# A streaming encoder trunk: product 7's bank read at once, the first loads in order of need, and two multiplications of the last unit on GpSimd

## The chip, the core and the metric

The kernel runs on one core of a Trainium2 chip. The metric is the device time of one launch in microseconds (us). The core's engines are TensorE (PE; PEld is its weight load), VectorE (DVE), ScalarE (ACT), GpSimd (POOL) and SyncE (SP), which issues most DMAs. They have their own instruction queues and wait for each other by semaphores. Products are summed in PSUM, in banks of 128x512 f32.

## The reference, cut to what matters

One layer of a trunk over 2048 prompt tokens and 32 sample tokens, width 1024, all in f32:

```
h  = rmsnorm(x, g_pre_mix);  z = h @ w_in             # u | q | f | i | g, 512 columns each
y  = concat(pool_mix(u), hgrn(q, f, i) * silu(g)) @ w_out
x1 = x + rmsnorm(y, g_post_mix)
h2 = rmsnorm(x1, g_pre_ffn)
f  = (silu(h2 @ w_gate) * (h2 @ w_up)) @ w_down        # 2816 hidden columns
x2 = x1 + rmsnorm(f, g_post_ffn)
rmsnorm(x, g) = x * rsqrt(mean(x*x) + 1e-6) * g
```

`pool_mix` is a trailing mean with a small product per group, `hgrn` a gated recurrence evaluated in chunks. Outputs are x2 of both groups and the last pool rows and states.

## The kernel before, in words

The prompt is worked in two halves of 1024 tokens, the samples with the second. Each f32 product is made of three matmuls of f32r operands: every operand is split in a part `hi` (a ScalarE cast) and a rest `lo` (a VectorE subtraction), and hi·hi, hi·lo and lo·hi are summed in one bank.

**The start.** `first_values` (L566) makes the i columns of z for the first half. Everything in it, on all engines, stands in program order (`tc.manual_schedule`, L1732); in the rest of the kernel only TensorE's order is written out, and a planner orders the other engines by its own costs. The function issues its loads on SP: channel block 0 of x (`xT`, in two halves), weight rows 0 and 1 (`wrow`), channel block 1, then for `kp` 1 to 3 two channel blocks (512 KB, `channel_load`, L445) and two blocks of weight rows (512 KB, `raw_rows2`, L257), then constants (L592) and token tiles (`xt`, L451). Each channel block is scaled and split (`unscaled`, L595 to 601), each weight block split, and TensorE makes four tiles of 12 matmuls in all per channel block. Between blocks 5 and 6 stand the `rb` products (L504): they spread the roots of the tokens' mean squares, which come from the token tiles by ScalarE (`sumsq`, L319), GpSimd (L325, L326) and VectorE (`dg`, L461).

**Gate and up.** `gate_up` (L1246) makes gate and up columns by seven products per matrix m, in the manner of Strassen-Winograd, with 22 matrices in each half, gate and up in turn. Products 1, 6, 5 and 3 sum on in one bank `M.x` (`gx`); product 7 opens the bank `M.y` (`gy`) and product 4 sums on in it. So the value that product 7 alone leaves in `M.y` has to be read before product 4, and what product 5 leaves in `M.x` before product 3. A matrix is `held` when `M.x` starts with product 1 (m under 4 or from 6 on); in the others the copy `p1` is added by hand. The order is written out in `order_of` (L1179): 7, 5, product 1 of the next matrix, 4, 3, 6, 2 in the common run, and at the end of the stage, for the last matrices a and b, products 6, 2, 7, 5, 4, 3 of a and b in turn. `later` (L1255) holds steps that are emitted at the beginning of the next product's step.

**Down.** `down` (L1544) takes the hidden columns through seven products again, adding to `acc` in SBUF. In the last group each finished half row of a token tile goes to `half_done` (L1583): sum of squares on ScalarE, and in the very last unit (`direct`) at once the multiplication by the norm weight, `fg`. When both halves are there, GpSimd makes the root (`rstd_of`, L323, L326) and `done` (L1605) scales, adds the residual and stores. The last unit's order is 6, 7, 5, 4, 2, 3: its second tile t + 4 is finished by products 5 and 4, its first tile t by 2 and 3.

Of the kernel before, what the change touches and what calls it, by code (L numbers as in the profile page):

```python
# [13 lines left out]
ALU = mybir.AluOpType  # L14
PSUM = bass.MemoryType.PSUM

P = 128
# [61 lines left out]
def body(tc, ins, outs, cst):  # L79
    nc = tc.nc  # L80
    ctx = ExitStack()
    with ctx:
# [9 lines left out]
        def ztile(name, shape=None, dt=F32):  # L92
            return UP.tile(shape or [P, SLOT], dt, tag="u", name=name)
# [13 lines left out]
        def t2(name, shape=None, dt=F32):  # L107
            return TP.tile(shape or [P, 512], dt, tag="t", name=name)
# [7 lines left out]
        x_t = ins["x_channels"].rearrange("(k p) t -> p k t", p=P)  # L116
        w_in = ins["w_in"][0]
# [72 lines left out]
        class Pace:  # L190
            t = 0.0
# [80 lines left out]
        def raws(n):  # L272
            its = Stream.items
            while Stream.nraw < min(n, len(its)):
                its[Stream.nraw] = its[Stream.nraw]()
                Stream.nraw += 1
# [146 lines left out]
        COL_Q, COL_F, COL_I, COL_G = 512, 1024, 1536, 2048  # L423
# [19 lines left out]
        def channel_load(S, tg, k, n):  # L443
            t0 = S.tok0 + tg * 512
            nc.sync.dma_start(out=S.xT[tg][k // 2][:, k % 2:k % 2 + n], in_=x_t[:, k:k + n, t0:t0 + 512])  # L445
# [120 lines left out]
        def first_values(S):  # L566
# [7 lines left out]
            front_loads(S)  # L574
            S.xT[0] = [ztile("xT", [P, 2, 512]) for _ in range(4)]
            for kp in range(4):
                if kp:
                    channel_load(S, 0, 2 * kp, 2)
                    raws(kp + 1)
                    continue  # L580
                x0 = x_t[:, 0, S.tok0:S.tok0 + 512]
                nc.sync.dma_start(out=S.xT[0][0][:, 0, 0:256], in_=x0[:, 0:256])
                raw = ztile("wrow", [P, 2 * 512])
                Stream.items[0] = lambda: raw
                for i in range(2):
                    nc.sync.dma_start(out=raw[:, i * 512:(i + 1) * 512], in_=w_in[i * P:(i + 1) * P, COL_I:COL_I + 512])
                    if i == 0:
                        nc.sync.dma_start(out=S.xT[0][0][:, 0, 256:512], in_=x0[:, 256:512])
                    else:
                        channel_load(S, 0, 1, 1)  # L590
                raws(1)
# [18 lines left out]
            raw = Stream.items[0]  # L610
# [12 lines left out]
            for k in range(0, KD, 2):  # L623
# [9 lines left out]
                for kk in range(2):  # L633
# [9 lines left out]
                    if k + kk == KD - 3:  # L643
                        later = scaled_channels(S, 1)
# [601 lines left out]
        def gate_up(S, on_last):  # L1246
# [8 lines left out]
            jobs, later, gs = [], [], {}  # L1255
# [55 lines left out]
            def product(M, p, ps, start):  # L1311
                while p not in S.F:
                    S.post[1].step()
                wf, F = M.f.pop(p), S.F[p]
                for k in (0, 2):
                    trios = [(*(wf[:, i, kk * P:(kk + 1) * P] for i in range(2)),
                              *(x[:, (kk % 2) * 512:(kk % 2) * 512 + 512] for x in F[kk // 2])) for kk in (k, k + 1)]
                    for n, (a, b) in enumerate(in_turn(trios)):
                        mm(ps, a, b, start and k == 0 and n == 0, k == 2 and n == 5, rcost(512), not start)
                        if n % 3 == 2:  # L1320
                            poll()

            def close(M, name):
                c = getattr(M, name)
                if M.gate is None:
                    later.append(lambda: nc.scalar.activation(c, c, AF.Silu))
                else:
                    nc.vector.tensor_tensor(c, c, getattr(M.gate, name), ALU.mult)
# [24 lines left out]
            def step(m, p):  # L1353
                M = mats[m]
                if p == 1:
                    M.gate = mats[m - 1] if m % 2 else None
                    M.x = mmbank("gx") if M.held else axbank("gw")
                    product(M, 1, M.x, True)
                    M.c11 = t2("c11")
                    nc.scalar.copy(M.c11, M.x)  # L1360
                    if not M.held:
                        M.p1, M.c11 = M.c11, t2("c11")
                elif p == 2:
                    if M.held:
                        z = axbank("gz")
                        product(M, 2, z, True)
                        nc.vector.tensor_tensor(M.c11, z, M.c11, ALU.add)
                        close(M, "c11")
                    else:
                        product(M, 2, M.x, False)  # L1370
                        if M.gate is None:
                            nc.scalar.activation(M.c11, M.x, AF.Silu)
                        else:
                            nc.vector.tensor_tensor(M.c11, M.x, M.gate.c11, ALU.mult)
                elif p == 6:
                    if not M.held:
                        M.x = mmbank("gx")
                    product(M, 6, M.x, not M.held)
                    M.c21 = t2("c21")
                    if M.held:  # L1380
                        nc.scalar.copy(M.c21, M.x)
                    else:
                        nc.vector.tensor_tensor(M.c21, M.x, M.p1, ALU.add)
                    if m == len(mats) - 1:
                        sampled([m - 1, m])
                elif p == 7:
                    M.y = axbank("gy")
                    product(M, 7, M.y, True)
                elif p == 5:
                    product(M, 5, M.x, False)  # L1390
                    M.c22 = t2("c22")
                    if M.held:
                        nc.scalar.copy(M.c22, M.x)
                    else:
                        nc.vector.tensor_tensor(M.c22, M.x, M.p1, ALU.add)
                    if m < LEAD:
                        if m % 2:
                            sampled([m - 1, m])
                    elif m < len(mats) - 2 and m % 2 == 0:
                        sampled([m, m + 1])  # L1400

                    def rest():
                        nc.vector.tensor_tensor(M.c22, M.y, M.c22, ALU.add)  # L1403
                        close(M, "c22")
                    later.append(rest)
                elif p == 4:
                    product(M, 4, M.y, False)
                    nc.vector.tensor_tensor(M.c21, M.y, M.c21, ALU.add)
                    close(M, "c21")
                else:  # L1410
                    product(M, 3, M.x, False)
                    M.c12 = t2("c12")
                    src = M.x
                    if not M.held:
                        src = M.c12
                        nc.vector.tensor_tensor(M.c12, M.x, M.p1, ALU.add)
                        M.p1 = None
                    if M.gate is None:
                        nc.scalar.activation(M.c12, src, AF.Silu)
                    else:  # L1420
                        nc.vector.tensor_tensor(M.c12, src, M.gate.c12, ALU.mult)
                        jobs.append(hidden(S, m // 2, [M.c11, M.c12, M.c21, M.c22]))
                        mats[m - 1] = mats[m] = None
# [62 lines left out]
        class Down:  # L1486
            w = [None] * len(GROUPS)
# [56 lines left out]
        def down(halves):  # L1544
# [6 lines left out]
            gpf = []  # L1551
# [31 lines left out]
            def half_done(t, dh, direct):  # L1583
                cs = slice(dh * 512, dh * 512 + 512)
                f = acc[t][:, cs]
                if t not in stats:
                    xh = None
                    if direct:
                        xh = ztile("x1r", [P, D])
                        nc.sync.dma_start(out=xh, in_=x1_rows(t * P, P))  # L1590
                    stats[t] = [new_stat(), [], xh, [t2("fg") for _ in range(2)] if direct else None]
                st, seen, xh, fg = stats[t]
                sumsq(f, P, st[:, dh:dh + 1])
                seen.append(dh)
                if direct:
                    nc.vector.tensor_tensor(fg[dh], f, gpf[0][:, cs], ALU.mult)
                if len(seen) == 1:
                    first_half(st, P, dh)
                else:
                    rstd_of(st, P, True, nc.gpsimd, dh)  # L1600
                    for i in range(2):
                        wait = 1 if direct else i + (3 if t % 8 > 3 else 4)
                        pending.append((slot[0] + wait, lambda i=i: done(t, direct, i)))
# [192 lines left out]
```

## Time and profile before

| what | value |
|---|---|
| timed runs | median 2088.18 us (2087.85 to 2088.67, 3 runs) |
| profiled execution, own time | 2086.21 us |
| its span, first to last instruction | 2084.4 us |
| mean granted TensorE clock | 0.998 |
| PE / DVE / ACT / POOL busy | 99% / 68% / 40% / 14% |
| DMA | 321.06 MB, mean 154 GB/s |

The span is cut by stage: the first values until about 53 us, heads, pools and projection of the first half until 377, its gate and up until 800, the second half's mixers until 1187, its gate and up until 1640, down until 2075, and the tail. In the rows, a line reads start, duration, engine, line, operation, `out<-in`, shapes; what stands in brackets is the idle time before it and what ended it. TensorE's matmuls all carry line L199, that of a helper, so they are told apart by tile: `vps` first values, `rb` roots, `gx`, `gy`, `gz` gate and up, `dx`, `dy`, `dz` down.

### The profile page before, as it was taken

Reading aid. Unit: us, or ns where it says so; the run is one execution under the profiler, and the core shown is the slowest. Engines: PE = TensorE matmul, PEld = TensorE weight load, DVE = VectorE, ACT = ScalarE, POOL = GpSimd, SP = SyncE. Lnnn points to the kernel's source line nnn. Section 1 sums busy time; section 2 is a strip of 40 time slices with the busy share of each in tenths; the row PEclk is TensorE's granted clock in tenths of the full one; section 3 lists DMA queues with packets and bytes.
Section 4 is the critical chain, followed back from the end, with each engine's and each line's share of the span. In section 5 each row is a group of like instructions: output and inputs, shape, how many; then the busy total and the mean of one; then the engine's idle time right before and its main releaser. Section 6 shows DMA issues by size and latency. Waiting matters only on the chain.

```text
span 2084.4 us, 34134 instructions
## 1 busy us (share of the span) xinstructions
PE 2071.4 (99%) x13112; PEld 1689.0 (81%) x13112; DVE 1423.6 (68%) x2303; ACT 830.7 (40%) x1661; POOL 281.9 (14%) x387
## 2 busy tenths in 40 slices
PE   9999999999999999999999999999999999999998
PEld 8788888888888888788888788888888778888876
DVE  6566765787776778365575697776666766566587
ACT  6444445654444445233334563444444521011032
POOL 1133302100000000122231200000000210110133
PEclk9999999999999999999999999999999999999999
DMA  9321144435555558211014614554445796776778
GB/s 326 112 72 52 45 142 144 150 115 174 157 162 147 158 171 262 72 46 36 25 54 174 202 50 138 163 149 144 142 138 171 237 326 208 216 225 207 213 225 213
DMA packets 393361, 321.06 MB, mean 154 GB/s; under 512 B 18128, under 2 KB 320720, under 8 KB 393200
## 3 DMA queue, kind: packets, MB, share of 16 engines
q1 hardware_dynamic: 390752, 310.98, 48.1%
q0 software_dynamic: 2016, 7.34, 1.9%
q8 instruction: 103, 1.69, 0.3%
q10 hardware_dynamic: 432, 0.57, 0.1%
q14 instruction: 58, 0.48, 0.1%
HBM read 218.36 MB, written 100.47 MB: 153 GB/s over the span
## 4 chain that ended last, share of the span: by engine, by line
PE 94%; DVE 3%; issue 1%; ACT 1%; DMA 0%; POOL 0%; SPq 0%; DVEq 0%; POOLq 0%; ACTq 0%
PE gx L199 22%; PE mmb L199 16%; PE gy L199 11%; PE dx L199 10%; PE ops L199 10%; PE gz L199 5%; PE dy L199 5%; PE vps L199 4%; PE dz L199 3%; PE gb L199 1%; PE gw L199 1%; PE gsps L199 1%; DVE acc L1581 1%; PE ups L199 1%; PE tps L342 1%
## 5 line engine op out<-in xcount | busy, mean ns | idle before, releaser
L199 PE MATMUL gx<-fhi,wf 128*128 128x512 f32 x1376 | 387.0, 391 | 0.0
L199 PEld LDWEIGHTS gx<-fhi,wf 128*128 128x128 f32 x1376 | 256.7, 188 | 55.0 <-issue 2.2
L199 PE MATMUL gx<-flo,wf 128*128 128x512 f32 x688 | 213.1, 390 | 0.0
L199 PE MATMUL gy<-fhi,wf 128*128 128x512 f32 x704 | 201.6, 390 | 1.0 <-DVE c L1403 1.0
L199 PE MATMUL dx<-dhi,hst 128*128 128x512 f32 x640 | 185.3, 391 | 1.0 <-DVE acc L1581 0.9
L199 PE MATMUL mmb<-hTlo,whi 128*128 128x512 f32 x512 | 176.3, 405 | 0.0
L199 PE MATMUL mmb<-hThi,whi 128*128 128x512 f32 x512 | 165.8, 405 | 0.0
L1581 DVE TENSOR_TENSOR acc<-dx,acc 128x512 f32<-128x512 f32 x168 | 115.0, 689 | 71.3 <-PE dx L199 70.3
L199 PE MATMUL mmb<-hThi,wlo 128*128 128x512 f32 x512 | 159.0, 392 | 0.0
L1301 DVE TENSOR_TENSOR wf<-s,wf 128x512 fp32r<-128x512 f32 x176 | 119.7, 687 | 56.1 <-ACT wf L1296 54.2
L199 PEld LDWEIGHTS gy<-fhi,wf 128*128 128x128 f32 x704 | 131.8, 188 | 29.1 <-DVE c L1403 1.4
L199 PEld LDWEIGHTS gx<-flo,wf 128*128 128x128 f32 x688 | 129.1, 188 | 27.0
L1296 ACT CAST wf<-s 128x512 fp32r<-128x512 f32 x176 | 107.9, 621 | 102.3 <-DVE s L1277 31.5
L199 PEld LDWEIGHTS dx<-dhi,hst 128*128 128x128 f32 x640 | 119.6, 188 | 30.2 <-issue 3.4
L1520 ACT CAST dhi<-t 128x1024 fp32r<-128x1024 f32 x20 | 20.7, 1053 | 250.7 <-DVE dlo L1521 182.4
L1301 DVE TENSOR_TENSOR wf<-wraw,wf 128x512 fp32r<-128x512 f32 x132 | 89.6, 686 | 34.4 <-ACT wf L1296 34.4
L199 PEld LDWEIGHTS mmb<-hTlo,whi 128*128 128x128 f32 x512 | 96.2, 188 | 20.8 <-issue 1.3
L199 PEld LDWEIGHTS mmb<-hThi,wlo 128*128 128x128 f32 x512 | 96.3, 188 | 19.3 <-issue 0.7
L1296 ACT CAST wf<-wraw 128x512 fp32r<-128x512 f32 x132 | 80.7, 621 | 76.0 <-PE gx L199 36.3
L199 PEld LDWEIGHTS mmb<-hThi,whi 128*128 128x128 f32 x512 | 91.8, 188 | 21.1 <-issue 3.8
L199 PE MATMUL gy<-flo,wf 128*128 128x512 f32 x352 | 108.7, 389 | 0.0
L199 PE MATMUL dx<-dlo,hst 128*128 128x512 f32 x320 | 98.7, 389 | 0.0
(333 smaller groups left out, 3995.0 us busy)
## 6 DMA issues: line engine op xcount, KB each, us to landing
hst<-hdFalse SPq DMA_DIRECT2D x140, 256.0 KB, 2.9
hst<-hdTrue SPq DMA_DIRECT2D x140, 256.0 KB, 2.9
wraw<-in_w_gate_dram SPq DMA_DIRECT2D x50, 512.0 KB, 4.0
wraw<-in_w_up_dram SPq DMA_DIRECT2D x50, 512.0 KB, 4.0
hdFalse<-hhi SPq DMA_DIRECT2D x77, 256.0 KB, 2.3
hdFalse<-hlo SPq DMA_DIRECT2D x77, 256.0 KB, 2.3
hdTrue<-hhi SPq DMA_DIRECT2D x77, 256.0 KB, 2.6
hdTrue<-hlo SPq DMA_DIRECT2D x77, 256.0 KB, 2.6
```

The lines of the kernel that those rows point to most:

```text
L199: nc.tensor.matmul(out, l, r, start=start, stop=stop, skip_group_check=more)
L342: nc.tensor.transpose(ps[:, c:c + P], xn[:, (2 * kp + kk) * P:(2 * kp + kk + 1) * P], ident)
L1296: nc.scalar.copy(wf[:, 0], getattr(M, src) if isinstance(src, str) else src)
L1301: nc.vector.tensor_tensor(wf[:, 1], getattr(M, src) if isinstance(src, str) else src, wf[:, 0].bitcast(F32), ALU.subtract)
L1520: nc.scalar.copy(hi, src)
L1581: nc.vector.tensor_tensor(dst, ps, dst, ALU.add)
```

## The change

Three edits. In `first_values` the loads of `kp` 1 are issued as four DMAs of 256 KB in the order channel block 2, weight block 2, channel block 3, weight block 3, and GpSimd copies one column into the destination of three DMAs first, from a block that has to have landed: weight block 0 before channel block 2, weight block 1 before channel block 3, channel block 1 before channel blocks 4 and 5. As the DMA writes over that column, it is held until the copy is done. In `gate_up` `c22` is begun after product 7 from `M.y`, and `M.x` is added to it after product 5; the deferred `rest` is gone. In `half_done` the `fg` of tiles with t % 8 > 3 (in the last unit the second tile) goes from VectorE to GpSimd.

```diff
--- before.py
+++ after.py
@@ -574,7 +574,21 @@
             front_loads(S)
             S.xT[0] = [ztile("xT", [P, 2, 512]) for _ in range(4)]
             for kp in range(4):
+                if kp == 1:
+
+                    raw = ztile("wrow", [P, 2 * 512])
+                    Stream.items[1] = lambda: raw
+                    seen = Stream.items[0][:, 0:1], Stream.items[0][:, 512:513]
+                    for i in range(2):
+                        x, w = S.xT[0][1][:, i], raw[:, i * 512:(i + 1) * 512]
+                        nc.gpsimd.tensor_copy(x[:, 0:1], seen[i])
+                        nc.sync.dma_start(out=x, in_=x_t[:, 2 + i, S.tok0:S.tok0 + 512])
+                        nc.sync.dma_start(out=w, in_=w_in[(2 + i) * P:(3 + i) * P, COL_I:COL_I + 512])
+                    raws(2)
+                    continue
                 if kp:
+                    if kp == 2:
+                        nc.gpsimd.tensor_copy(S.xT[0][2][:, 0, 0:1], S.xT[0][0][:, 1, 0:1])
                     channel_load(S, 0, 2 * kp, 2)
                     raws(kp + 1)
                     continue
@@ -1386,23 +1400,20 @@
                 elif p == 7:
                     M.y = axbank("gy")
                     product(M, 7, M.y, True)
+                    M.c22 = t2("c22")
+                    if M.held:
+                        nc.scalar.copy(M.c22, M.y)
+                    else:
+                        nc.vector.tensor_tensor(M.c22, M.y, M.p1, ALU.add)
                 elif p == 5:
                     product(M, 5, M.x, False)
-                    M.c22 = t2("c22")
-                    if M.held:
-                        nc.scalar.copy(M.c22, M.x)
-                    else:
-                        nc.vector.tensor_tensor(M.c22, M.x, M.p1, ALU.add)
+                    nc.vector.tensor_tensor(M.c22, M.x, M.c22, ALU.add)
                     if m < LEAD:
                         if m % 2:
                             sampled([m - 1, m])
                     elif m < len(mats) - 2 and m % 2 == 0:
                         sampled([m, m + 1])
-
-                    def rest():
-                        nc.vector.tensor_tensor(M.c22, M.y, M.c22, ALU.add)
-                        close(M, "c22")
-                    later.append(rest)
+                    later.append(lambda: close(M, "c22"))
                 elif p == 4:
                     product(M, 4, M.y, False)
                     nc.vector.tensor_tensor(M.c21, M.y, M.c21, ALU.add)
@@ -1593,7 +1604,7 @@
                 sumsq(f, P, st[:, dh:dh + 1])
                 seen.append(dh)
                 if direct:
-                    nc.vector.tensor_tensor(fg[dh], f, gpf[0][:, cs], ALU.mult)
+                    (nc.gpsimd if t % 8 > 3 else nc.vector).tensor_tensor(fg[dh], f, gpf[0][:, cs], ALU.mult)
                 if len(seen) == 1:
                     first_half(st, P, dh)
                 else:
```

## Rows read from the trace of the kernel before

**Rows 1.** The page, busy time per engine: us (share of the span), instructions.

```profile
PE 2071.4 (99%) x13112; PEld 1689.0 (81%) x13112; DVE 1423.6 (68%) x2303; ACT 830.7 (40%) x1661; POOL 281.9 (14%) x387
```

**Rows 2.** Windows of three stages: us, busy time (instructions) per engine, clock, DMA.

```profile
377.00:800.00 423.00, 423.00 (x1883) 349.98 (x1882) 329.62 (x511) 209.07 (x364) 10.87 (x19) 1.00 0.53 156
...
1187.00:1640.00 453.00, 452.02 (x2637) 372.56 (x2634) 336.58 (x522) 210.34 (x375) 22.49 (x24) 1.00 0.49 145
1640.00:2075.00 435.00, 434.00 (x1939) 348.57 (x1938) 280.78 (x392) 81.15 (x144) 75.62 (x81) 1.00 0.78 234
```

**Rows 3.** Waits of TensorE: engine, line, waited for, us in total, times, longest.

```profile
PE gy L199 <- DVE c L1403: 1.0, 1, 1.0
```

**Rows 4.** Chain of waits, 0 to 60 us: start, us, what.

```profile
2.58 5.61 DMA xT<-x_channels
...
24.52 24.50 PE vps L199 x108
```

**Rows 5.** Timeline of the tail: start, us, instruction, idle before it and its releaser.

```profile
2072.16 0.69 DVE L1596 TENSOR_TENSOR fg<-acc,gv 128x512 f32<-128x512 f32 x1
...
2074.44 0.27 POOL L323 TENSOR_SCALAR st<-st 128x1 f32<-128x1 f32 x1 [1.21 <-ACT junk L319]
...
2074.78 0.61 PE L199 MATMUL dx<-dhi,hst 128*128 128x512 f32 x2
2074.79 0.56 POOL L326 TENSOR_TENSOR st<-st,nhalf 128x1 f32<-128x1 f32 x1
...
2075.38 0.75 DVE L1609 SCALAR_TENSOR_TENSOR acc<-fg,st,x1r 128x512 f32<-128x512 f32 x1 [0.60 <-POOL st L326]
...
2076.05 0.68 DVE L1596 TENSOR_TENSOR fg<-acc,gv 128x512 f32<-128x512 f32 x1
...
2077.32 0.68 DVE L1581 TENSOR_TENSOR acc<-dx,acc 128x512 f32<-128x512 f32 x1
```

**Rows 6.** Timeline of the seam between gate/up and down of the second half.

```profile
1625.65 0.57 ACT L1393 COPY c<-gx 128x512 f32<-128x512 f32 x1
...
1627.13 1.28 DVE L1301 TENSOR_TENSOR wf<-s,wf 128x512 fp32r<-128x512 f32 x2
...
1628.94 0.68 DVE L1403 TENSOR_TENSOR c<-gy,c 128x512 f32<-128x512 f32 x1
...
1629.67 0.73 PE L199 MATMUL gy<-fhi,wf 128*128 128x512 f32 x2 [0.98 <-DVE c L1403]
...
1632.25 2.72 POOL L1508 TENSOR_TENSOR t<-wdr,t 128x1024 f32<-128x1024 f32 x1
1632.64 2.88 DVE L1328 TENSOR_TENSOR c<-c,c 128x512 f32<-128x512 f32 x1
```

**Rows 7.** Groups of GpSimd instructions by line.

```profile
L1041 POOL COPY kds<-es 128x15 f32<-128x15 f32 x4 | 1.3, 317 | 15.3 <-DVE es L1008 15.3
```

**Rows 8.** Timeline of the start.

```profile
8.98 0.50 PE L199 MATMUL vps<-whw,xg 128*128 128x512 f32 x1 [0.32 <-ACT xg L600]
...
9.77 0.74 PE L199 MATMUL vps<-whw,xg 128*128 128x512 f32 x2
...
16.13 1.14 ACT L236 CAST whw<-wrow 128x512 fp32r<-128x512 f32 x2 [0.23 <-DMA wrow<-in_w_in_dram]
...
23.69 0.29 DVE L461 TENSOR_SCALAR dg<-cons,st 128x128 f32<-128x128 f32 x1 [0.96 <-POOL st L326]
```

**Rows 9.** Token tiles' DMAs (L451), 0 to 14 us: durations ns, starts; issue to landing.

```profile
L451 SPq DMA_DIRECT2D xt<-in_x_prompt_dram x4: 327/328/340, 8.2 to 12.3; - x4
...
DMA to landing us min/median/max: 9.3/9.3/9.3
```

**Rows 10.** Windows of the start; the last column is GB/s, before it DMA share.

```profile
10.00:16.00 6.00, 6.00 (x27) 4.76 (x27) 5.12 (x8) 5.14 (x9) 0.00 (x0) 1.00 1.05 411
```

**Rows 11.** Line L1507 of GpSimd: duration ns min/median/max, first and last start, shapes.

```profile
L1507 POOL TENSOR_TENSOR t<-wdr x6: 1357/2400/2418, 1614.6 to 1927.5; 128x1024 f32<-128x1024 f32 x5, 128x512 f32<-128x512 f32 x1
```

**Rows 12.** Line L1581 of VectorE, the adds from PSUM, same columns.

```profile
L1581 DVE TENSOR_TENSOR acc<-dx,acc x168: 669/691/692, 1645.3 to 2077.3; 128x512 f32<-128x512 f32 x168
```

## Prediction

> **What bounds the kernel now.** First the page's busy times: TensorE works 2071.4 of 2084.4 us [rows 1], so an edit can win only inside the 13 us that are left, or lose by opening new gaps. Then the busy time by stretch, to place those 13 us: the reader is to see TensorE at 423.00 of 423.00 us in the first gate/up stage, 452.02 of 453.00 in the second and 434.00 of 435.00 in the down stage [rows 2]. The waits of TensorE name the missing 0.98 of the second: one wait, product 7's bank `gy` on VectorE's L1403 [rows 3]. The chain of waits shows the start: the DMA of the second channel block lands at 2.58 + 5.61 = 8.19, and at 24.52, where the norm row products `rb` are done, 108 matmuls begin that follow without a gap in 24.50 us, 0.227 us each [rows 4]. The timeline of the tail shows the end: the last matmuls stop at 2074.78 + 0.61 = 2075.4, and 9.0 us of VectorE, ScalarE, GpSimd and the output DMA follow [rows 5]. So there are three places, and each edit touches one.
>
> **Part A, the bank of product 7.** For each of 44 matrices the edit moves one bank copy (by ScalarE; a VectorE add for the 4 unheld) from product 5's bank to product 7's, a step or two earlier, and lets the VectorE add read product 5's bank right after it. Counts and shapes stay: one copy, one add. What goes is product 4's dependence on an add that stands late in VectorE's queue. At the seam the copy of product 5 is done at 1625.65 + 0.57 = 1626.22, but L1403 stands behind two L1301 (from 1627.13) and what follows them, runs at 1628.94, and product 4 starts at 1629.67 after 0.98 of idle [rows 6]. With the edit product 4 needs only the copy of product 7's bank. The order there is 7a 7b 5a 5b 4a, so that copy has three products of time, 36 x 0.227 = 8.2 us. What is late next? Product 3 overwrites product 5's bank, now read by VectorE: three products lie between them here, two (5.4 us) in the ordinary order. The weights of product 4 are split five steps ahead. I take the whole 0.98, and since the down stage behind it has 1 us of gaps in 435 [rows 2], it is carried to the end. Bounds: 0, if another late VectorE operation takes the spot, and 0.98. The cost: tile c22 lives one or two steps (2.7 to 5.4 us) longer in a pool of 21. A first stage without any gap in 423 us says that buffers are not short; without that cover a late buffer costs a slip of the matmuls at some of 44 places, and 0.1 us at each would be 4.4 us, kept as a tail of the range.
>
> **Part B, the first loads.** The second pair of channel blocks and weight rows goes from two DMAs of 512 KB to four of 256 KB, and three GpSimd copies of one column hold DMAs back until the first weight block, the second weight block and the second channel block have landed. The nearest row for such a copy is 0.317 us (128x15) [rows 7]. Behind each held DMA stands the whole SP queue: the other blocks, the constants, the token tiles.
> What it can win: block 1 lands at 8.19, its first matmul starts at 8.98 after 0.32 idle, and the third at 9.77 [rows 8]. Two matmuls of 0.227 need 0.45 of those 0.79, so 0.34 more is lost: 0.66 in all. If block 1 lands a microsecond sooner, TensorE reaches `rb` 0.66 earlier.
> But `rb` needs four sums of squares. The fourth `dg` runs at 23.69 [rows 8], after the fourth token tile, which is issued at 12.3 and lands 9.3 us later, at 21.6 [rows 9]; and ScalarE's casts before it wait for weights to the last (0.23 at 16.13) [rows 8]. From 10 to 16 us the DMA engines are saturated at 411 GB/s [rows 10]: this stretch hangs on bytes, and the bytes stay. An earlier TensorE waits at `rb` and leaves it at 24.52 again. So I take 0. Gain bound: 0.66 and ScalarE's 0.23, 0.9 us, if the whole stream comes sooner. Loss bound: if block 1 still lands at 8.19, the third and fourth pairs are issued only from 8.19 + 0.32 on, and after four issues of about 0.45 us the token tiles start at 10.3, not at 8.2: 2.1 us. But a DMA issued there waits 9.3 us in a queue [rows 9], most of which is other blocks' bytes, so a later issue costs nothing while the queue is not empty; 0 is nearer to that row than 2.1.
> The Trainium skill has a rule on this ("DMA: Bandwidth & Descriptors", section "Queues, rings and completion order"): on each engine the descriptors of a queue are consumed in ring order. By that rule later blocks cannot pass block 1 on an engine, holding them back would not land it sooner, part B's gain bound would be 0, and the best case below would end at 2085.6. The 5.61 us of the row do not decide it, and no row here shows the order on one engine.
>
> **Part C, the tail.** Two multiplications of 0.69 (`fg` of the second tile, the first at 2072.16) leave VectorE, which waits for matmuls between them anyway: hidden, worth 0. On GpSimd the nearest row is 1.357 for 128x512 f32 with two inputs (L1507's minimum, its one instruction of that shape) [rows 11]. GpSimd then runs: 2072.16 + 1.36 = 2073.52; a small statistic (priced at the 0.27 of its sister step) to 2073.8; the second multiplication to 2075.2; the two root steps (0.27 and 0.56, with gaps) to about 2076.1, where the root ended at 2074.79 + 0.56 = 2075.35 [rows 5]. On that root hangs the scale of the second tile (L1609) at 2075.38; behind it in VectorE's queue stand `fg` of the first tile at 2076.05, the other L1609, and only at 2077.32 the add of the last product, whose matmuls ended at 2075.4. From that add 7.1 us lead to the end.
> In the same order VectorE waits to 2076.1: +0.7. If `fg` of the first tile goes first (2074.8, when VectorE is idle), then both L1609 from 2076.1 (1.3), the add comes at 2077.5: +0.2. If the add goes ahead of the L1609s too, it comes at about 2075.5, 1.8 earlier, and is done at 2076.2; then the two L1609s (1.4) and the last `fg` (0.7) fill VectorE to 2078.3, where the last pair of L1609 begins, now at 2079.91: -1.6. The program order of VectorE is a planner's, by its own costs, and a later root makes it put other ready work ahead: I take +0.2, the middle case, and keep -1.6 and +0.7.
> There is a second price. Beside a GpSimd operation of 2.72 us a VectorE operation with both inputs in SBUF took 2.88 [rows 6], where adds with a PSUM input took 0.692 at most in all 168 [rows 12]. The tail's adds are of the second kind; of the first is `fg` of the first tile, which would wait from 2074.8 to 2075.2 and still end before 2076.1: 0.
>
> **Sum.** -0.98 + 0 + 0.2 = -0.8. The profiled execution took 2086.21 us around its span of 2084.4, and would take 2085.4. It lies 1.97 below the median 2088.18 of the three timed runs (2087.85 to 2088.67), and the change takes the same from both: 2087.4.
>
> **Rivals.**
> 1. The held DMAs let the queue run empty (slower): three waits in series, in a stretch that hangs on bytes, with `rb` behind the last byte. Against it stand 9.3 us of queued work. At the bound: -0.98 + 2.1 + 0.2 = +1.3, 2089.5. From a loss of 0.8 us on it outweighs the rest.
> 2. The tail keeps VectorE's order and GpSimd becomes the late engine: -0.98 + 0.7 = -0.3, 2087.9. For it: 1.36 replaces 0.69 and the root stands behind it. Against it: a late root lets other work go ahead.
> 3. All three gain: -0.98 - 0.9 - 1.6 = -3.5, 2084.7; with the tail alone, -2.6, 2085.6. For it: 1.9 us of the last add's delay are pure queue order. Against it: both need more than the edit itself, a stream of bytes that comes sooner and a luckier order.
> 4. Product 4 stalls on something else at the seam, and the change does not do what it says: 0 + 0.2, 2088.4. Against it: the wait has L1403 alone as its end.
>
> **How the numbers follow.** Forecast 38%, rival 1 17%, rival 2 15%, rival 3 20%, rival 4 6%, buffer pressure 4% (at 4.4 - 0.8 = +3.6, 2091.8, or more). The forecast's own band is 2086.6 to 2088.2, as runs of one kernel differ by 0.8. For 8 in 10 the range takes in rivals 2 to 4 and most of rival 1: 2084.6 to 2089.8. About 0.2% (4.2 us) is what a measurement of this kernel can tell from no change. Below 2084.0 lies only the pile-up of every gain with a low run: 6%. Above 2092.4 lie half of the buffer case and a start that loses more than its bound: 6%. Within: 88%.
>
> **What would show it.** A: no wait of `gy` near 1628, and TensorE busy all 453 us of that stage. B: block 1 landing before 8.19 and `rb` still done at 24.5; wrong if it is done before 24.0 or after 25.2. C: from the last matmul to the end, 9.0 now, 9.2 forecast; 7.4 or 9.7 name the other orders. All of it is wrong if gaps over 1 us appear between 377 and 1640.

## The result, and the profile after

The changed kernel took 2092.82 us (median of 11 runs, 2091.82 to 2094.03) beside 2087.85 for the kernel before (11 runs, 2086.70 to 2089.94): ratio 1.0024 [1.0016, 1.0031], 5.0 us slower, with 3.3 to 6.5 as the interval. The forecast was 0.8 us faster. The profiled execution took 2091.82 us around a span of 2089.9, 5.5 more than the span of before.

Marks along TensorE's order tell where the 5.5 us came in. Each difference is against the same mark of before, and the last column is what the stretch ending there added:

| mark | before | after | later by | this stretch |
|---|---|---|---|---|
| first `mmb` matmul, the first values done | 52.64 | 55.79 | 3.15 | +3.15 |
| first `gx` of the first half | 377.58 | 380.99 | 3.41 | +0.26 |
| first `gx` of the second half | 1187.38 | 1192.66 | 5.28 | +1.87 |
| end of the last matmul | 2075.40 | 2079.73 | 4.33 | -0.95 |
| end of the span | 2084.4 | 2089.9 | 5.5 | +1.17 |

So part A's gain is there (-0.95) and three losses stand against it: the start, a seam in the middle where nothing was edited by hand, and the tail.

**The page and the windows.** Busy time per engine, then the two gate and up stages of [rows 2], moved by the delays above:

```profile
PE 2072.8 (99%) x13112; PEld 1690.2 (81%) x13112; DVE 1422.0 (68%) x2301; ACT 829.0 (40%) x1661; POOL 284.9 (14%) x392
```

```profile
380.00:804.00 424.00, 424.00 (x1889) 351.09 (x1888) 328.88 (x511) 208.21 (x364) 11.40 (x20) 1.00 0.52 155
1192.00:1645.00 453.00, 453.00 (x2645) 373.24 (x2638) 336.51 (x524) 210.41 (x376) 22.02 (x24) 1.00 0.49 145
```

The second line is the one that part A was to fill, and it is full. TensorE's busy time rose by 1.4 us (2071.4 in [rows 1]) for the same 13112 matmuls: somewhere matmuls became slower.

**The waits of TensorE**, in the columns of [rows 3]:

```profile
PE rb L199 <- DVE dg L461: 2.5, 3, 1.3
PE vps L199 <- ACT va L714: 1.4, 1, 1.4
...
PE gb L199 <- ACT f_t L879: 0.8, 3, 0.4
```

The wait of `gy` is gone. New are 2.5 us at `rb` in the start and 1.4 at `vps` near 827.

**The start.** The chain of waits ([rows 4] is its counterpart):

```profile
5.92 0.31 POOL xT L584
...
7.14 6.13 DMA xT<-x_channels
...
13.29 9.82 DMA xt<-in_x_prompt_dram
...
25.28 0.30 DVE dg L461
...
25.63 0.79 PE rb L199 x2
26.42 25.74 PE vps L199 x108
```

The chain now runs over the second of the three copies that hold DMAs (5.92) and over a token tile issued late: the fourth was issued at 13.29 and landed 9.82 us later, at 23.11, where before it was issued at 12.3 and landed at 21.6 [rows 9]. The fourth `dg` comes at 25.28 instead of 23.69, `rb` is left at 26.42 instead of 24.52, and the 108 matmuls behind it take 25.74 instead of 24.50. The timeline of the same stretch shows the holds and the waits:

```profile
4.65 0.18 POOL L584 COPY xT<-wrow 128x1 f32<-128x1 f32 x1 [3.66 <-DMA wrow<-in_w_in_dram]
4.87 0.33 SPq L585 DMA_DIRECT2D xT<-x_channels  x1
...
6.24 0.33 SPq L585 DMA_DIRECT2D xT<-x_channels  x1
6.54 0.27 POOL L591 COPY xT<-xT 128x1 f32<-128x1 f32 x1 [0.33 <-DMA xT<-x_channels]
...
10.25 3.37 SPq L451 DMA_DIRECT2D xt<-in_x_prompt_dram  x4
...
21.76 0.38 PE L199 MATMUL rb<-dg,ones 128*128 128x128 f32 x2
...
22.61 0.49 PE L199 MATMUL rb<-dg,ones 128*128 128x128 f32 x2 [0.47 <-DVE dg L461]
...
25.63 0.79 PE L199 MATMUL rb<-dg,ones 128*128 128x128 f32 x2 [1.32 <-DVE dg L461]
...
27.07 1.05 PE L199 MATMUL vps<-whw,xg 128*128 128x512 f32 x2
```

SP issues nothing from 3.01 to 4.87 and from 5.67 to 6.24, while it waits for the first and the second copy; the third copy costs it under 0.1 us. Block 1 has landed by 6.54 (8.19 before), so TensorE reaches `rb` at 21.76, earlier than the 23.17 of before in the same view; but there it now waits three times (0.47, 0.72 and 1.32 us), since the token tiles are issued from 10.25 and not from 8.2. The last row has matmuls at half the pace. The windows say why (after the length of the window: busy TensorE, then the other engines, the granted clock, the DMA share, GB/s):

```profile
9.00:10.00 1.00, 1.00 (x6) 0.81 (x6) 1.00 (x2) 0.54 (x1) 0.00 (x0) 1.00 0.59 162
...
26.00:27.00 1.00, 1.00 (x4) 0.88 (x4) 0.54 (x1) 0.00 (x0) 0.00 (x0) 0.50 1.05 408
...
28.00:29.00 1.00, 1.00 (x4) 0.81 (x3) 0.98 (x2) 1.00 (x2) 0.00 (x0) 0.55 1.05 406
29.00:30.00 1.00, 1.00 (x6) 0.78 (x6) 0.74 (x2) 0.53 (x1) 0.00 (x0) 1.00 1.06 410
```

The first of these windows in the kernel before:

```profile
9.00:10.00 1.00, 0.94 (x3) 0.51 (x4) 0.72 (x1) 0.34 (x1) 0.00 (x0) 1.00 1.05 408
```

In the three microseconds from 8 us on the DMA rate is 272, 162 and 244 GB/s, where before it was 375, 408 and 410: the queue is no longer full. And after the waits at `rb` the granted clock is 0.50 to 0.55 for three microseconds, the lower of TensorE's two levels (1.2 GHz).

**The tail**, to be read beside [rows 5]:

```profile
2076.26 0.86 POOL L1625 DMA_DIRECT2D out_dram<-acc  x1 [1.58 <-DVE acc L1623]
...
2076.82 1.61 POOL L1607 TENSOR_TENSOR fg<-acc,gv 128x512 f32<-128x512 f32 x1
...
2078.80 1.28 POOL L1607 TENSOR_TENSOR fg<-acc,gv 128x512 f32<-128x512 f32 x1
...
2080.41 0.56 POOL L326 TENSOR_TENSOR st<-st,nhalf 128x1 f32<-128x1 f32 x1
2081.00 0.75 DVE L1620 SCALAR_TENSOR_TENSOR acc<-fg,st,x1r 128x512 f32<-128x512 f32 x1 [1.90 <-POOL st L326]
...
2081.67 0.69 DVE L1607 TENSOR_TENSOR fg<-acc,gv 128x512 f32<-128x512 f32 x1
...
2082.93 0.68 DVE L1592 TENSOR_TENSOR acc<-dx,acc 128x512 f32<-128x512 f32 x1
```

VectorE's order is that of before: scaling, `fg` of the first tile, scaling, and then the add of the last product. The root it waits for ends at 2080.97, 1.24 after the last matmul; before, it ended at 2075.35, with the last matmul.

### The profile page after: what moved, and what is told of

The parts are those of the page before. It is cut to its first block, busy times and chain, and to the rows that moved or that the text cites. A ratio compares the mean times of both kernels' runs of the same rounds, so it can differ in the third digit from the quotient of the medians.

```text
span 2089.9 us, 34130 instructions
## 1 busy us (share of the span) xinstructions
PE 2072.8 (99%) x13112; PEld 1690.2 (81%) x13112; DVE 1422.0 (68%) x2301; ACT 829.0 (40%) x1661; POOL 284.9 (14%) x392
## 4 chain that ended last, share of the span: by engine, by line
PE 91%; DVE 4%; DMA 2%; issue 1%; ACT 1%; POOL 1%; SPq 0%; DVEq 0%; POOLq 0%; ACTq 0%
PE gx L199 22%; PE mmb L199 16%; PE gy L199 11%; PE dx L199 10%; PE ops L199 10%; PE dy L199 5%; PE gz L199 5%; PE dz L199 3%; PE vps L199 2%; PE gb L199 1%; PE gw L199 1%; PE gsps L199 1%; DMA xT<-x_channels 1%; PE ups L199 1%; DVE acc L1592 1%
```

## The experiments

Each kernel is compared with the kernel before on the same chip, 11 runs against 33 (21 for the last two). Times of a stage are those of the one profiled execution.

### Each part alone

The three parts of the diff, one at a time (each the lines of that part as they stand in the diff above), and part B with four small products added between the `rb` products, so that TensorE is less idle there:

```diff
+                spare = axbank("warm") if tg == 1 else None
                 for i in range(4):
+                    for _ in range((0, 1, 1, 2)[i] if tg == 1 else 0):
+                        mm(spare[:, 0:P], ones, ones, True, True, 0.0)
```

> Only the bank of product 7 is read at once; first loads and tail as before. Theory 1 (each part keeps its own place): the 0.98 us wait of gy near 1628 is gone and nothing else moves: -1.0 us against before. Theory 2 (the rewritten step makes the planner order VectorE, ScalarE and SP otherwise, and the gap of 1.4 us that the changed kernel has between the halves, near 828, comes from that): the gap is here too, and the time is +0.4 to +0.9 us.

> Only the first loads are changed. Theory 1: the start loses what the changed kernel shows, rb left at about 26.4 instead of 24.5 and the 108 matmuls behind it in 25.7 instead of 24.5: +3.1 us at 55 us of the span, +3.1 to +3.5 in all, and no gap near 828. Theory 2 (the gap between the halves hangs on the changed start, through the plan): +4.5 to +5.3 in all, with a wait of about 1.4 us near 828. Rival to both (the start is made up later because something else bounds): within +1.

> Only the two multiplications of the last unit's second tile go to GpSimd. Theory 1: VectorE's order in the tail stays as before, the root of the second tile comes 1.2 to 1.3 us later behind the two multiplications, and the last add waits for it: from the last matmul to the end 10.2 instead of 9.0, +1.2 us. Rival (the tail is bound by the output DMA or the longer tail is noise of one execution): 0 to +0.3.

> The first loads as in the change, and between the four rb products four further 128x128 products of ones into a bank that nobody reads, which fill about 1.9 us of the 2.5 us in which TensorE waits there. Theory 1 (the granted clock falls to 1.2 GHz because TensorE idles at rb, and the 108 matmuls behind pay for it): the clock stays at 2.4 GHz, the 108 matmuls take 24.5 us again, and the time is 1.2 us less than with the changed loads alone, at +1.9. Rival (the clock falls for another reason, such as the pattern of loads): it falls again, and the time is that of the changed loads alone or up to 0.3 more.

| kernel | median us | ratio to before | difference us |
|---|---|---|---|
| part A alone | 2088.20 | 1.0003 [0.9994, 1.0012] | +0.4 |
| part B alone | 2091.72 | 1.0019 [1.0010, 1.0028] | +4.0 |
| part C alone | 2089.42 | 1.0006 [0.9997, 1.0015] | +1.7 |
| part B with the small products | 2090.43 | 1.0012 [1.0003, 1.0021] | +2.7 |

The parts add up to +6.1, with about 2 us of uncertainty in each; the whole is +5.0. Part B is most of it.

*Part B.* Alone it shows both steps of the start again; with the small products only the first. The chain of part B alone, and then with them:

```profile
25.90 0.49 PE rb L199 x2
26.39 26.15 PE vps L199 x108
```

```profile
25.74 0.49 PE rb L199 x2
26.23 24.51 PE vps L199 x108
```

`rb` is left at the same time, 26.4 and 26.2, but with the small products the 108 matmuls take 24.51, as before, and the granted clock from 26 to 28 is 1.00. The medians differ by 1.3 us; the intervals of the two kernels overlap, so the rows carry this step, and the medians agree with it. That the clock's fall costs 1.2 to 1.6 us on the 108 matmuls is shown by these rows. The expectation had the step itself right (24.5 us again, 1.2 us less) and the whole too low (+1.9; it was +2.7).

*Part A.* In part A alone the `gy` wait is gone, gate and up of the second half takes 452.37 us from its first `gx` to the first `dx` (453.37 before), and yet the median is not lower: from the start of the second half's `vps` to its first `gx` it takes 388.82 where before took 387.00. Its waits name the same seam as the whole change:

```profile
PE vps L199 <- ACT va L700: 1.2, 1, 1.2
```

The three other kernels of this group keep the old step, and their profiles show that its wait can cost more than its own length. In part B alone:

```profile
PE gy L199 <- DVE c L1417: 2.2, 1, 2.2
```

The wait is 2.2 us here and with the small products, and 1.8 in part C alone. In all three profiles the granted clock is then 0.54 to 0.61 for four microseconds, and the stage takes 457.3, 457.2 and 456.1 us, 2.8 to 3.9 more than before.

*Part C.* Its tail, last matmul to end, is 10.28 us, as in the whole change (10.17), and 9.0 before. The median (+1.7) is not apart from no change.

### Where part A loses, and which step of part B and C costs

Part A in the second half only; part B without the three copies that hold the DMAs; part B with `rb` one channel block later; part C with one of the tile's two multiplications on GpSimd.

```diff
 # A in the second half: at product 7, and in the same way at product 5
+                    if S.B:
+                        M.c22 = t2("c22")
...
 # B without holds, against the changed kernel
-                        nc.gpsimd.tensor_copy(x[:, 0:1], seen[i])
...
-                    if kp == 2:
-                        nc.gpsimd.tensor_copy(S.xT[0][2][:, 0, 0:1], S.xT[0][0][:, 1, 0:1])
 # B with rb later, against part B alone
-                    if k + kk == KD - 3:
+                    if k + kk == KD - 2:
 # C with one multiplication
-                    nc.vector.tensor_tensor(fg[dh], f, gpf[0][:, cs], ALU.mult)
+                    (nc.gpsimd if t % 8 > 3 and dh else nc.vector).tensor_tensor(fg[dh], f, gpf[0][:, cs], ALU.mult)
```

> Product 7's bank is read at once in the second half's gate and up only; the first half keeps the old step, loads and tail as before. Theory (the edit removes the gy wait at the seam into down, and in the first half only disturbs the planner's order, which gives the gap near 828): no wait of gy near 1628, no gap near 828, and -1 to -2 us, since that wait took 1.0 to 2.2 in the profiles so far. Rival (the gap near 828 comes by chance with any new plan, or the gy wait is made good elsewhere): a gap between 800 and 1187 of over 0.5 us again, or a time within 0.5 of before.

> The first loads in the new order and sizes (four DMAs of 256 KB for the second pair), but without the three GpSimd copies, so that no DMA is held. Theory (the holds let the DMA queue run empty between 9 and 11 us): SP issues without a pause, over 370 GB/s again from 9 us on, block 1 lands at about 8 as before, rb is left at 24.5, and the time is that of before, 0 to +0.5 us. Rival (the smaller DMAs or the order cost the stream, not the holds): rb left at 26 or later and +3 us.

> The first loads as in the change, and the four rb products one channel block later in TensorE's order, behind block 6 instead of block 5. Theory (the earlier block 1 wins 1.5 us of TensorE's time at the start, and it is lost only because rb stands in order ahead of work that is ready): TensorE does the 12 matmuls of block 6 (2.7 us) while the last token tile lands, waits 0 to 1.2 us at rb, the clock stays up, and the start is 0.3 to 0.8 us shorter than before, so the time is about 4 us below the changed loads alone: -0.8 to 0 against before. Rival (everything behind rb needs its result, so the wait only moves): rb as late, a new wait of 2 to 3 us on the next products, and +2 to +4.

> Of the last unit only the first multiplication (product 5's half row) goes to GpSimd, the other (product 4's) stays on VectorE. Theory (the tail is late because the second multiplication stands ahead of the root in GpSimd's queue, behind a first one delayed by a store that GpSimd issues): the root of the second tile ends 0.6 us after the last add's input as before, from the last matmul to the end 9.0 to 9.2, and the time is that of before, 0 to +0.2 us. Rival (any GpSimd multiplication beside the tail's VectorE work costs, by the store in front or by shared ports): 9.6 to 10.2 again.

| kernel | median us | ratio to before | difference us |
|---|---|---|---|
| A in the second half | 2086.85 | 0.9997 [0.9989, 1.0006] | -1.0 |
| B without holds | 2088.41 | 1.0002 [0.9993, 1.0011] | +0.6 |
| B with `rb` later | 2089.47 | 1.0009 [1.0000, 1.0017] | +1.7 |
| C with one multiplication | 2088.30 | 1.0004 [0.9995, 1.0013] | +0.5 |

*A in the second half* keeps the gain (452.35 us for gate and up) and loses the gap: 386.95 us from `vps` to `gx`, and no wait of TensorE in between. So the gap comes with the edit in the first half. SP's timeline tells what the edit did there. Before:

```profile
795.79 0.58 SPq L445 DMA_DIRECT2D xT<-x_channels  x1
799.61 0.37 SPq L1228 DMA_DIRECT2D hdFalse<-hlo  x1
...
800.95 1.40 SPq L445 DMA_DIRECT2D xT<-x_channels  x3
```

In the whole change:

```profile
803.39 0.37 SPq L1242 DMA_DIRECT2D hdFalse<-hlo  x1
...
805.09 2.24 SPq L445 DMA_DIRECT2D xT<-x_channels  x4
```

Four channel loads, which only read the input, now all stand behind the store of the last hidden block, which waits for gate and up to be finished; before, the first of them went ahead of it. VectorE waits for that load, and the chain of waits starts from it:

```profile
DVE xT L512 <- DMA xT<-x_channels: 5.6, 1, 5.6
```

```profile
805.09 6.62 DMA xT<-x_channels
```

Before, its wait at that line was 3.1 us and for the roots. From the landing at 811.7 the chain runs on through VectorE, with no pause above 0.6 us, to its copy `va` of a bank at 829.17. TensorE waits for that copy and for the one before it, which ScalarE makes behind its casts:

```profile
826.84 0.73 PE L199 MATMUL vps<-whw,hThi 128*128 128x512 f32 x2 [1.39 <-ACT va L714]
...
829.91 0.30 PEld L199 LDWEIGHTS vps<-whw,hThi 128*128 128x128 f32 x2 [0.48 <-DVE va L714]
```

The two waits, 1.39 and 0.48 us, are together the 1.87 of the table. In the first half itself the old step is not quite free: in this profile, which keeps it there, `gy` waits 0.63 us at 793; in the other eight with it there is no such wait.

*B without holds* gives most of the loss back (+0.6 against +4.0 with them):

```profile
9.00:10.00 1.00, 0.00 (x0) 0.00 (x0) 0.00 (x0) 0.74 (x2) 0.00 (x0) 1.00 1.03 399
```

DMA stands at 399 GB/s from 9 to 10 us and 412 in the next, and the 108 matmuls take 24.52. `rb` is left at 25.39 and block 1 lands at 2.58 + 6.66 = 9.24, both later than the expectation said (24.5 and about 8), but no later than in kernels whose start was not touched (see below). So the medians and the DMA rates put the cost on the holds, and not on the four smaller DMAs or their order.

*B with `rb` later* takes most of the waits at `rb` away (0.2 us are left), keeps the clock at its higher level through the start, and by the medians regains 2.3 of the 4.0 (the intervals of the two kernels overlap); in the profiles the first values are done 2.4 us earlier than in part B alone. A new wait of 1.7 takes part of the place:

```profile
PE vps L199 <- ACT va L662: 1.7, 1, 1.7
```

So the work behind `rb` is short of time too, and moving the wait doesn't remove most of it. Theory (-0.8 to 0) and rival (+2 to +4) were both missed; the larger part of what is regained is the clock's (1.65 in part B alone).

*C with one multiplication* has a tail of 9.39 us, between the 9.0 and the 10.2. In its tail the two engines multiply side by side:

```profile
2073.79 1.62 POOL L1596 TENSOR_TENSOR fg<-acc,gv 128x512 f32<-128x512 f32 x1
2074.75 1.22 DVE L1596 TENSOR_TENSOR fg<-acc,gv 128x512 f32<-128x512 f32 x1
```

VectorE's takes 1.22 us where it takes 0.69 alone: the price that the prediction had put at 0 for want of an operation beside it. It is not what lengthens this tail, though, since VectorE waits for the root afterwards:

```profile
2077.05 0.75 DVE L1609 SCALAR_TENSOR_TENSOR acc<-fg,st,x1r 128x512 f32<-128x512 f32 x1 [0.49 <-POOL st L326]
```

The root ends 0.31 us after the last matmul, where before it ended with it: one multiplication in front of it on GpSimd is enough to delay it, and the expected 9.0 to 9.2 was missed. In the whole change VectorE has only adds from PSUM beside GpSimd's multiplications, at their usual 0.69, so the second price does not fall due there.

### The other half of part A, and a version with a better tail

Part A in the first half only, and part A in the second half with the add of the last product put ahead of the second scaling:

```diff
 # A in the first half: at products 7 and 5
+                    if not S.B:
...
 # A in the second half, better tail: in half_done
-                        wait = 1 if direct else i + (3 if t % 8 > 3 else 4)
+                        wait = 2 if direct else i + (3 if t % 8 > 3 else 4)
```

> Product 7's bank is read at once in the first half's gate and up only; the second half, the loads and the tail are as before. Theory (in the first half the edit wins nothing, since TensorE never waits for gy in the middle of it, and the new order of SP puts the second half's channel loads behind a store of hidden columns): VectorE waits about 5 us for xT near 804, TensorE 1.2 us near 828, the gy wait near 1628 is there, and the time is +1.2 to +2 us. Rival (the gap near 828 is one execution's, or is made good at the next seam): within 0.5 of before.

> The second half alone reads product 7's bank at once, all multiplications stay on VectorE, and in the last unit the second tile's scaling is held one step longer, so that VectorE takes the last product's add ahead of the second L1609. Theory (the tail is bound by the order of VectorE's queue: the last add stands 1.9 us behind its matmuls): the add comes 0.6 to 0.7 us earlier, from the last matmul to the end 8.3 to 8.4 instead of 9.0, and the time is 1.6 us below before (1.0 from the bank, 0.65 from the tail), the fastest of all. Rival (the tail's end hangs on the output DMA of the second tile or on its root, not on the add): 8.9 to 9.0 and -1.0.

*A in the first half* took 2089.91 us, 1.0010 [1.0002, 1.0019], slower by 1.9, the only one of these four part A kernels that is apart from before. It has the seam's wait (2.5 us in its profile), the same order on SP with all four channel loads behind the store, 391.35 us from `vps` to `gx`, and the `gy` wait of the second half is back:

```profile
PE vps L199 <- ACT va L700: 2.5, 1, 2.5
...
PE gy L199 <- DVE c L1413: 1.0, 1, 1.0
```

The 391.35 is 4.35 above before, and the wait explains 2.5 of it. Behind the wait the granted clock falls, and the matmuls run at half the pace for some three and a half microseconds, which is about 1.7 of the other 1.85:

```profile
828.00:830.00 2.00, 2.00 (x6) 1.52 (x6) 2.00 (x5) 1.72 (x2) 0.00 (x0) 0.50 0.00 0
```

Half against half, the edit is worth about -1.0 in the second half (unresolved) and +1.9 in the first.

*The version with the better tail* took 2086.21 us, 0.9995 [0.9986, 1.0004], 1.8 less than before. The interval includes no change, so it is not shown to beat it. Its tail is 8.46 us, for the reason intended: the add of the last product starts at 2077.21, ahead of the second scaling.

```profile
2077.21 0.68 DVE L1591 TENSOR_TENSOR acc<-dx,acc 128x512 f32<-128x512 f32 x1
2077.81 0.74 DVE L1619 SCALAR_TENSOR_TENSOR acc<-fg,st,x1r 128x512 f32<-128x512 f32 x1
```

## Why the prediction was wrong

**Part A, -0.98: right, and not the whole.** The wait went, nothing else was late at the seam between gate/up and down, and the gain came out at the end of the stage as forecast (-0.95). In the kernels with the old step this stage took 453.4 to 457.3 us (eight profiles), in those with the new one 452.3 to 452.7 (four). The kernel before had the shortest of the eight: with a wait of 1.0 the stage takes 453.4 to 454.0, and the three above 456 are those in which the wait was 1.8 to 2.2 and the clock fell behind it. Those three ran on one chip, and four of the other five on others, so whether the chip or the execution decides is open. That forecast and gain agree so closely (0.98 and 0.95) is owed in part to comparing with the profile from which the forecast was read. The failed step is the price of the rest: "tile c22 lives one or two steps (2.7 to 5.4 us) longer", with late buffers as its only form. The prediction looked for a cost among the 44 places and the stages of gate and up, where there is none (424 of 424 us). The cost (+1.87) stood in the stage behind, at 827, and in another queue: with a changed step in the first half the planner put SP's channel loads behind the hidden store. The same text of the edit gains in the half where nothing of the sort stands behind it. "All of it is wrong if gaps over 1 us appear between 377 and 1640" named this sign, without its cause. All twelve profiles agree with the order on SP as the cause: in the three with the edit in the first half (the whole change, A alone, A in the first half) the four loads are behind the store, VectorE waits 5.2 to 6.3 us for the first of them, and TensorE's wait of 1.2 to 2.5 us is there; in the nine without it the first load goes ahead and there is no such wait. The edit also changes VectorE's order in that half, and a kernel with the old order of SP held by hand was not tried: that the edit in the first half costs this is shown, that SP's order alone does it is read from the chain.

**Part B, 0: wrong in two steps.** The first is "a later issue costs nothing while the queue is not empty". The condition was right and taken as met on one row: a token tile's 9.3 us from issue to landing [rows 9]. But that row is of before, where nothing holds the queue; the holds themselves take out what filled it. From 4 to 13 us the DMA engines moved 347 GB/s before and 279 after; the first line is before, the second after:

```profile
4.00:13.00 9.00, 8.62 (x34) 6.27 (x34) 5.11 (x9) 5.62 (x10) 0.00 (x0) 1.00 1.00 347
```

```profile
4.00:13.00 9.00, 8.90 (x40) 7.32 (x40) 5.03 (x9) 5.43 (x9) 0.76 (x3) 1.00 0.82 279
```

The four profiles with the holds have 254 to 279 there, the eight without 321 to 347. 68 GB/s over 9 us is 0.61 MB, and at 411 GB/s that is 1.5 us: the 1.5 by which the fourth token tile lands later. Of the 1.9 by which `rb` is left later, 1.6 is the later `dg`, and 0.3 is that the last `rb` products took 0.79 us instead of 0.49, the clock already falling. That is rival 1 with its mechanism. That its bound of 2.1 is near the 1.9 is partly luck: the bound put the delay on the third hold, with block 1 landing at 8.19, while block 1 landed by 6.54, the third hold cost nothing, and the first two, which the prediction gave no time, made the token tiles start at 10.25. The bound was worked out, put in the text, and then set aside for a row that the edit changes.
The second step was not in the text at all. "An earlier TensorE waits at `rb`" was held to be free. It waited 2.5 us, and then worked for three microseconds at the lower level of its clock: +1.24 on the 108 matmuls in the profile of the change, +1.65 in that of part B alone. The start thus cost 3.15 against the one profile of before, half again as much as the largest loss that the prediction allowed for it.
Of what block 1's delay was worth (0.66 in the prediction; TensorE reached `rb` 1.4 earlier) nothing is left at the end, as forecast, for the reason forecast: the earlier matmuls only wait longer at `rb`.
The rule of the Trainium skill that was weighed ("DMA: Bandwidth & Descriptors", section "Queues, rings and completion order") stands apart from these numbers. It says in which order descriptors are consumed, and adds that a later one may finish its write before an earlier one; that holding later blocks back would not land block 1 sooner was the prediction's own step. The traces go against that step: block 1 had landed by 6.5 to 7.0 us in the four profiles with the holds, and landed at 7.4 to 9.5 in the eight without, at 9.24 with the same four smaller DMAs. Whether the order on one engine is kept, as the rule states, no run here shows; that later blocks delay an earlier one, these times do.

**Part C, +0.2: the mechanism of rival 2, larger.** The failed step is the choice of the middle case, "a later root makes it put other ready work ahead". It did not: VectorE's order stayed, so the add of the last product waits for the root. The size was off too. The root was forecast 0.7 later than before and came 1.29 later on the scale of the last matmul: GpSimd's queue held a store issue (2076.26) in front of the first multiplication, which began some 0.3 later than VectorE's had, and that multiplication took 1.61 where 1.36 was assumed from L1507 [rows 11]. The second took 1.28. So 0.7 became 1.3 at the root and 1.2 at the end, and the tail, for which 9.2, 7.4 and 9.7 were to tell the orders apart, read 10.17: the unchanged order, with a later root.

**Put together,** the prediction's parts came out at -0.95 + 3.15 + 1.17 = +3.4, and the seam (+1.87) and the heads (+0.26) were in no part. Corrected for the two mechanisms it had named, rivals 1 and 2 at once with -0.98 + 1.9 + 1.2 = +2.1, it would still have missed the clock and the seam, the other 3.4 of the 5.5.

**What stays open.** The heads' +0.26 (the wait at `gb` is 0.8 in all four profiles with the holds and 0.5 in the eight without) was not followed up; part A alone, without holds, has +0.28 there. And the start differs by itself: in seven profiles with the start of before unchanged, `rb` was left at 24.23 to 27.00 (mean 25.4), block 1 landing from 7.4 to 9.5. The two latest, 26.77 and 27.00, later than any with the holds, are the two in which TensorE waited 1.8 and 1.9 us for block 1 near 9 us and the granted clock was then 0.50 from 12 to 14 us: the clock has a share in this spread too. The profile on which the prediction rests was one of the quicker ones. So the 1.9 measured against it may be about 1.0 against the mean, and the 3.15 of the start about 2.2; with the clock's 1.2 to 1.6 and 0.3 for the heads, part B's rows give 2.5 to 2.9 of its +4.0 [2.1, 5.8]. The remainder lies inside the interval and has no row.

## What to carry to other kernels

Price a hold on a DMA queue by what the queue would have carried in that time, not by the time a transfer took in the trace without the hold: a latency read from a full queue is no proof that the queue stays full once issues are held back. Where a planner orders the queues, an edit of one step is an edit of all of them: look after it for independent loads that have fallen behind a store or another late instruction, first at the seam behind the edited stage. A wait of TensorE can also cost more than its length: read the granted clock behind it before pricing it. And work moved to an idle engine joins that engine's queue: count what already stands in it, and ask whether the end of the moved work gates anything before pricing it as hidden.

## What the runs showed of the hardware

- In the changed kernel TensorE was at 1.00 of its clock until the waits at `rb` (0.47, 0.72 and 1.32 us, with two small products after each of the first two); it was granted 0.74 on the mean from 25 to 26 us, 0.50 to 0.55 (1.2 GHz) from 26 to 29, and 1.00 again from 29 on. With four more small products among the waits it stayed at 1.00. The price on the 108 matmuls was 1.24 us here and 1.65 in part B alone.
- The same fall stands behind single waits elsewhere: 1.8 and 1.9 us in the start of A in the second half and A in the first half, 1.8 to 2.2 at `gy` in part C alone, part B alone and part B with the small products, 2.5 at `va` in A in the first half. At `va` the lower clock cost about 1.7 us on top of the wait.
- The DMA engines moved 254 to 279 GB/s from 4 to 13 us in the four profiles with the holds, 321 to 347 in the eight without.
- A GpSimd multiplication of 128x512 f32 took 1.28 or 1.61 us, and a VectorE one with both inputs in SBUF, beside it, 1.22 where it took 0.69 alone. VectorE's adds with an input in PSUM stayed at 0.69 beside it.
- The same instructions at the start of the launch ended up to 2.8 us apart from execution to execution (`rb` left at 24.23 to 27.00).
